# Output projection of a hybrid attention and mLSTM layer: seven block products by Strassen's scheme instead of eight

## The chip, the cores and the metric

One NeuronCore of a Trainium2 chip. The metric is the device time of one execution in microseconds. The engines are named as the profile names them: PE (TensorE), DVE (VectorE), ACT (ScalarE), POOL (GpSimd), SP (SyncE, whose queue issues the DMAs here).

## The reference

A pre-RMSNorm layer on 4096 tokens of 1024 channels, in float32. One input projection feeds two groups of heads: stick-breaking attention (8 heads of 64) and mLSTM (4 heads of 128). Each branch is multiplied by a SiLU gate; the two are concatenated to `mix` (4096 x 1024). What the change touches is only the end:

```python
mix = jnp.concatenate([sb_out, ml_out], axis=-1)
h = h + mix @ w_out[layer].astype(mix.dtype)      # 4096x1024 @ 1024x1024
return rms_norm(h, final_norm_g)
```

## The kernel before

The program works through four sweeps over the tokens and then the output projection. Two sweeps do attention, two do mLSTM (two heads each); a sweep has 8 blocks of 512 tokens. An attention block has 8 slots, an mLSTM block 10. In an mLSTM block the slots 0 to 5 each hold one `t_quantum` (24 float16 matmuls of 512 columns), slots 6 to 9 each two `n_mm` groups (48 matmuls of 256 columns). All big products are split products: each operand is a high and a low part, and three of the four part products are summed (high x high, low x high, high x low).

The order is written out by hand. `at(slot, phase, fn)` hangs a function on the phase "pre", "mid" or "post" of a slot, `run` calls what hangs there, and each engine executes its own instructions in exactly the order in which they are issued. So an instruction that waits holds up everything behind it on its engine. Slot 0 of the projection is `c_g`, the last mLSTM block begins at `gl = c_g - 10`; work of a block trails into the next one's slots (`m2`, `m3`, `m3b`, `m4` of a block run in slots 0 to 5 of the next).

In those trailing slots DVE has a chain that TensorE waits for when it is late. In slot 2 `fin_conv` multiplies three times (L778); `m3` computes per-token statistics, on which POOL builds `rs` (L879, L880); in slot 3 `m3b` normalises (L886, four instructions), then come the next three multiplies, and in slot 4 `m4` transposes the first head on TensorE (L894) into the one PSUM buffer "at" and DVE reads it with the gate (L896). The second head's transposes in slot 5 need that buffer back, and all matmuls of the slot stand behind them. POOL meanwhile has the splits of weights (`split`, L251; `Prep.lows`, L314).

The projection (line 1125) takes a token tile of 128 rows and one half of the 1024 output columns at a time: 8 k-tiles x 3 part products = 24 matmuls of 512 columns with float32r operands, into one of two PSUM buffers "pj". `c_add` adds the result to x (L1130, DVE) and squares it for the norm (L1131, ACT). `c_norm` (L1170, L1171, POOL) makes the factor, `c_out` (L1178, DVE) scales the two halves and SP stores the tile. `m_load` fetches `mix` from the DRAM scratch `scr_m`, `m_split` makes its two parts (L250 ACT, L251 DVE). The weights are loaded and split in eight pieces in the last mLSTM block (`wo_load`: ACT and POOL, 1,024 wide, slots 2 to 9). The last tile's second half is done in two pieces of 256 columns (`c_last`) so that little is left behind the last matmul.

Of the kernel before, what the change touches and what calls it, by code (L numbers as in the profile page):

```python
# [43 lines left out]
def hymba_kernel(ctx: ExitStack, tc: tile.TileContext, x, norm_g, w_in, b_ig, b_fg, conv_w,
                 conv_b, hn_g, w_out, fn_g, out):
    nc = tc.nc
    x2, out2 = x[0], out[0]
# [151 lines left out]
def main_pass(ctx, tc, x2, norm_g, win, win_k, b_ig, b_fg, conv_w, conv_b, hn_g, wout_k, fn_g,  # L199
              out2, scr_u, scr_m, scr_M, scr_E, flag):  # L200
# [848 lines left out]
    WO = {}  # L1049
    gl = ml_g(2 * NB - 1)  # L1050

    def wo_load(i):
        box = []

        def ld():
            r = stage()
            half, k0 = (1, 2 * i) if i < 4 else (0, 2 * i - 8)
            SP.dma_start(out=r.rearrange("p (k c) -> p k c", k=2), in_=wout_k[:, k0:k0 + 2, 512 * half:512 * half + 512])
            box.append(r)

        def sp():
            key = ("ba"[i // 4], i % 4)
            if i < 6:
                WO[key] = [wp.tile([128, DM], F32R, tag="wT", name="wT", bufs=T_SLOTS) for _ in range(2)]
# [29 lines left out]
    mt = {}  # L1094

    def m_load(i):
        if i < 4:
            t = stage().rearrange("p (k t) -> p k t", k=KT)
            SP.dma_start(out=t, in_=scr_m[i])
            for j in range(2):  # L1100
                mt[i, j] = t[:, 4 * j:4 * j + 4, :]
            return
        for j in range(2):
            t = ph_tile("z", [128, 4, 128])
            SP.dma_start(out=t, in_=scr_m[i, :, 4 * j:4 * j + 4, :])
            mt[i, j] = t

    mb = {}

    def m_split(i):  # L1110
        if i // 2 not in mb:
            mb.pop(i // 2 - 2, None)
            mb[i // 2] = up.tile([128, 2, 2, KT, 128], F32R, tag="U", name="U", bufs=2)
        u = mb[i // 2][:, i % 2]
        for j in range(2):
            ks = slice(4 * j, 4 * j + 4)
            split(u[:, 0, ks, :], u[:, 1, ks, :], mt.pop((i, j)))

    def c_mm(ps, i, half, c0, n, mid=None):
        u = mb[i // 2][:, i % 2]  # L1120
        for k in range(KT):
            wh, wl = WO["ab"[half], k // 2]
            cs = slice((k % 2) * 512 + c0, (k % 2) * 512 + c0 + n)
            for j, (a, w) in enumerate(((0, wh), (1, wh), (0, wl))):
                PE.matmul(ps, u[:, a, k, :], w[:, cs], start=(k == 0 and j == 0), stop=(k == KT - 1 and j == 2))  # L1125
            if k == 3 and mid:
                mid()

    def c_add(ps, hsl, sq):
        V.tensor_tensor(out=hsl, in0=ps, in1=hsl, op=ALU.add)  # L1130
        A.activation(out=ph_tile("kl0", list(hsl.shape)), in_=hsl, func=AF.Square, scale=DM ** -0.5, accum_out=sq)  # L1131

    def c_quantum(g, i, half):
        run(g, "pre")
        ps = ps_tile("pj", [128, 512])
        c_mm(ps, i, half, 0, 512, lambda: run(g, "mid"))
        if i not in hs2:
            hs2[i] = sm.tile([128, 2], F32, tag="hs2", name="hs2", bufs=3)
        c_add(ps, xt[i][:, half * 512:(half + 1) * 512], hs2[i][:, half:half + 1])
        run(g, "post")  # L1140

    def c_last(g):

        run(g, "pre")
        i = NT - 1
        t, sq = xt.pop(i), hs2.pop(i)
        last = sm.tile([128, 1], F32, tag="ss", name="ss")
        y = ph_tile("kl1", [128, 512])
        for c0, dst in ((0, sq[:, 0:1]), (256, last)):
            ps = ps_tile("pj", [128, 256])  # L1150
            c_mm(ps, i, 0, c0, 256)
            c_add(ps, t[:, c0:c0 + 256], dst)
            if c0 == 0:
                G.tensor_scalar(out=sq[:, 0:1], in0=sq[:, 0:1], scalar1=sq[:, 1:2], scalar2=EPS, op0=ALU.add, op1=ALU.add)
                G.tensor_tensor(out=t[:, 512:1024], in0=t[:, 512:1024], in1=fng[1], op=ALU.mult)
            V.tensor_tensor(out=y[:, c0:c0 + 256], in0=t[:, c0:c0 + 256], in1=fng[0][:, c0:c0 + 256], op=ALU.mult)
        V.tensor_tensor(out=last, in0=last, in1=sq[:, 0:1], op=ALU.add)
        G.tensor_tensor(out=last, in0=last, in1=mhalf[:, 0:1], op=ALU.pow)
        V.tensor_scalar(out=y, in0=y, scalar1=last, scalar2=None, op0=ALU.mult)
        SP.dma_start(out=out2[i * 128:(i + 1) * 128, 0:512], in_=y)  # L1160
        A.activation(out=t[:, 512:1024], in_=t[:, 512:1024], func=AF.Copy, scale=last)
        SP.dma_start(out=out2[i * 128:(i + 1) * 128, 512:1024], in_=t[:, 512:1024])
        run(g, "mid")
        run(g, "post")

    def c_norm(i):
        t = xt[i]
# [4 lines left out]
        xt[i] = (t, ss)  # L1172

    def c_out(i):
# [4 lines left out]
        SP.dma_start(out=out2[i * 128:(i + 1) * 128, :], in_=t)  # L1179


    with tc.manual_schedule():
# [146 lines left out]
        seq = [(0, 1), (1, 1), (0, 0), (1, 0)]  # L1329
        for i in range(2, NT):  # L1330
            seq += [(i, 1), (i, 0)]
        where = {ih: n for n, ih in enumerate(seq)}
        load_fng()
        for i in range(NT):
            n = max(where[i, 0], where[i, 1])
            n_first = min(where[i, 0], where[i, 1])
            at(c_g + max(n_first - 2, 0), "pre", lambda i=i: x_load(i))
            if i < NT - 1:
                at(c_g + n + 1, "pre", lambda i=i: c_norm(i))
                at(c_g + n + 2, "pre", lambda i=i: c_out(i))  # L1340
            if i >= 4:
                at(c_g + 2 * i - 6, "pre", lambda i=i: m_load(i))
                at(c_g + 2 * i - 4, "mid", lambda i=i: m_split(i))

# [6 lines left out]
        for n, (i, half) in enumerate(seq[:-1]):  # L1351
            c_quantum(c_g + n, i, half)
        c_last(c_g + len(seq) - 1)
        for g in range(c_g + len(seq), c_g + len(seq) + 4):
# [31 lines left out]
```

## Time and profile before

| | |
|---|---|
| median of 3 timed runs | 2305.04 us (2304.14 to 2309.72) |
| profiled execution | 2303.64 us, of it 2301.9 us span |
| PE busy | 2211.8 us (96%), granted clock 0.986 in the mean |
| DVE, ACT, POOL busy | 1319.9, 1007.7, 719.3 us (57%, 44%, 31%) |

These lines of the page cut the span into 40 equal slices (57.5 us each); a digit is the busy share in tenths. The projection is the last six to seven slices.

```profile
PE   4699999999999999999999999999999999999998
PEld 3366566666666666567767665666667677888887
DVE  6477777756666666755555555654544445433332
ACT  3477667656666666533333333222333334222221
POOL 2277667754555556511111112200000013100000
PEclk7899999999999999999999999999999999999999
DMA  6244444411111122112222232221222224444442
```

TensorE is busy nearly everywhere, the other engines have room, and the DMA engines too. An engine's busy share does not say whether its next instruction comes in time for another engine; that is read from the timeline.

### The profile page before, as it was taken

Reading aid. Unit: us, or ns where it says so; the run is one execution under the profiler, and the core shown is the slowest. Engines: PE = TensorE matmul, PEld = TensorE weight load, DVE = VectorE, ACT = ScalarE, POOL = GpSimd, SP = SyncE. Lnnn points to the kernel's source line nnn. Section 1 sums busy time; section 2 is a strip of 40 time slices with the busy share of each in tenths; the row PEclk is TensorE's granted clock in tenths of the full one; section 3 lists DMA queues with packets and bytes.
Section 4 is the critical chain, followed back from the end, with each engine's and each line's share of the span. In section 5 each row is a group of like instructions: output and inputs, shape, how many; then the busy total and the mean of one; then the engine's idle time right before and its main releaser. Section 6 shows DMA issues by size and latency. Waiting matters only on the chain.

```text
span 2301.9 us, 36279 instructions
## 1 busy us (share of the span) xinstructions
PE 2211.8 (96%) x13945; PEld 1526.6 (66%) x13945; DVE 1319.9 (57%) x2725; ACT 1007.7 (44%) x1806; POOL 719.3 (31%) x1134
## 2 busy tenths in 40 slices
PE   4699999999999999999999999999999999999998
PEld 3366566666666666567767665666667677888887
DVE  6477777756666666755555555654544445433332
ACT  3477667656666666533333333222333334222221
POOL 2277667754555556511111112200000013100000
PEclk7899999999999999999999999999999999999999
DMA  6244444411111122112222232221222224444442
GB/s 184 52 90 93 93 98 97 112 46 47 65 57 56 56 67 84 59 51 74 74 74 74 74 92 47 65 65 57 60 55 65 61 74 138 146 138 150 152 137 93
DMA packets 221917, 193.98 MB, mean 84 GB/s; under 512 B 108084, under 2 KB 177768, under 8 KB 221736
## 3 DMA queue, kind: packets, MB, share of 16 engines
q1 hardware_dynamic: 221720, 191.59, 29.4%
q8 instruction: 111, 1.82, 0.3%
q14 instruction: 70, 0.57, 0.1%
q10 hardware_dynamic: 16, 0.00, 0.0%
HBM read 141.09 MB, written 50.46 MB: 83 GB/s over the span
## 4 chain that ended last, share of the span: by engine, by line
PE 73%; DVE 6%; issue 1%; ACT 1%; DMA 0%; POOL 0%; POOLq 0%; DVEq 0%; ACTq 0%
PE ps_pj L480 31%; PE ps_pj L492 17%; PE ps_pj L1125 15%; PE ps_zu L823 1%; DVE z L778 1%; PE ps_at L617 1%; PE ps_o L633 1%; PE ps_zu L866 1%; PE ps_zu L867 1%; DVE c L738 1%; PE ps_at L824 1%; PE ps_o L848 1%; PE ps_zu L848 1%; PE ps_at L894 1%; PE ps_zu L586 1%
## 5 line engine op out<-in xcount | busy, mean ns | idle before, releaser
L480 PE MATMUL ps_pj<-U,wT 128*128 128x512 f16 x4608 | 1045.0, 382 | 0.0
L480 PEld LDWEIGHTS <-wT 128*128 128x128 f16 x4608 | 452.5, 99 | 494.4 <-issue 11.4
L492 PEld LDWEIGHTS <-U 128*128 128x128 f16 x4608 | 452.1, 98 | 82.8 <-DVE kl L565 11.9
L492 PE MATMUL ps_pj<-wna,U 128*128 128x256 f16 (+1 forms) x3072 | 361.7, 276 | 17.4 <-DVE kl L565 7.5
L1125 PE MATMUL ps_pj<-wT,U 128*128 128x512 f32 (+1 forms) x1164 | 267.8, 387 | 0.0
L1125 PEld LDWEIGHTS ps_pj<-wT,U 128*128 128x128 f32 x1164 | 216.6, 188 | 44.3
L601 POOL TENSOR_TENSOR sA<-sA,bP 128x510 f32<-128x510 f32 x128 | 151.7, 1185 | 199.2 <-DVE bP L600 180.4
L600 DVE TENSOR_TENSOR_SCAN bP<-bP,D 128x512 f32<-128x512 f32 x128 | 162.9, 1273 | 53.1 <-POOL bP L592 52.9
L492 PE MATMUL ps_pj<-wnb,U 128*128 128x256 f16 x1536 | 178.1, 273 | 0.0
L1131 ACT ACTIVATE kl<-st 128x512 f32<-128x512 f32 (+1 forms) x65 | 40.7, 625 | 274.1 <-DVE st L1130 265.8
L879 POOL TENSOR_SCALAR rs<-mv 128x4 f32<-128x4 f32 x32 | 8.0, 250 | 483.7 <-DVE kl L773 448.4
L774 ACT ACTIVATE kl<-ps_pj,SC 128x512 f32<-128x512 f32 x64 | 44.0, 687 | 242.0 <-PE ps_pj L480 208.9
L1130 DVE TENSOR_TENSOR st<-ps_pj,st 128x512 f32<-128x512 f32 (+1 forms) x65 | 44.4, 683 | 173.9 <-PE ps_pj L1125 170.7
L825 DVE TENSOR_TENSOR bP<-ps_zu,bP 128x512 f32<-128x512 f32 x32 | 22.1, 691 | 203.5 <-PE ps_at L824 202.4
L778 DVE SCALAR_TENSOR_TENSOR z<-kl,CT,z 128x512 f32<-128x512 f32 x144 | 118.3, 821 | 19.8 <-ACT z L775 15.2
L622 DVE SCALAR_TENSOR_TENSOR ATl<-ps_at,ATh 128x512 f16<-128x512 f32 (+1 forms) x128 | 87.8, 686 | 41.3 <-ACT ATh L621 39.2
L810 POOL TENSOR_SCALAR_AFFINE_SELECT bP<-bP 128x512 f32<-128x512 f32 x32 | 24.3, 760 | 270.0 <-DVE bP L809 239.8
L787 ACT ACTIVATE v<-ps_pj,SC 128x256 f32<-128x256 f32 x64 | 30.3, 474 | 168.8 <-PE ps_pj L492 168.2
L1170 POOL TENSOR_SCALAR ss<-hs 128x1 f32<-128x1 f32 x31 | 9.6, 311 | 292.3 <-ACT kl L1131 292.3
L563 ACT ACTIVATE kh<-ps_pj 64x512 f16<-64x512 f32 x128 | 75.6, 590 | 57.4 <-PE ps_pj L480 39.1
L1125 PE MATMUL ps_pj<-wna,U 128*128 128x512 f32 (+1 forms) x396 | 92.8, 383 | 0.0
L537 ACT ACTIVATE zml<-ps_pj,SC 128x512 f32<-128x512 f32 x32 | 22.0, 687 | 159.8 <-DMA scr_m<-zml 144.8
(233 smaller groups left out, 3458.8 us busy)
## 6 DMA issues: line engine op xcount, KB each, us to landing
U<-scr_u SPq DMA_DIRECT2D x96, 512.0 KB
st<-in_x_dram SPq DMA_DIRECT2D x40, 512.0 KB
scr_u<-U SPq DMA_DIRECT2D x32, 512.0 KB
out_dram<-st SPq DMA_DIRECT2D x31, 512.0 KB
st<-in_w_in_dram SPq DMA_DIRECT2D x28, 512.0 KB
z<-scr_m SPq DMA_DIRECT2D x56, 256.0 KB
st<-in_x_dram SPq DMA_DIRECT2D x96, 128.0 KB
scr_m<-z SPq DMA_DIRECT2D x32, 256.0 KB
```

Of the source, the lines that this page charges most:

```text
L480: PE.matmul(p3, wt[:, a, k, :], u[:, :, b, k, :], start=(k == 0 and i == 0), stop=(k == KT - 1 and i == 2))
L492: PE.matmul(ps[:, c0:c0 + n], u[:, a, k, :], w[:, b, k, 0:n], start=first and j == 0, stop=last and j == len(order) - 1)
L563: A.activation(out=kh[d, h, 128:640], in_=ps[e], func=AF.Copy, scale=S_QKV)
L600: V.tensor_tensor_scan(out=bf, data0=bf, data1=D1[:, ::-1], initial=1.0, op0=ALU.mult, op1=ALU.max)
L601: G.tensor_tensor(out=sg[:, :, 0:255], in0=sg[:, :, 0:255], in1=b[:, :, 1:256], op=ALU.mult)
L622: V.scalar_tensor_tensor(out=l[:, i:, :], in0=ps[:, i:, :], scalar=S_A, in1=h[:, i:, :], op0=ALU.mult, op1=ALU.subtract)
L774: A.activation(out=raw[:, 3:515], in_=ps, func=AF.Copy, scale=inv(sid))
L778: V.scalar_tensor_tensor(out=y, in0=raw[:, t:t + 512], scalar=CT[:, 8 * t + grp:8 * t + grp + 1], in1=y, op0=ALU.mult, op1=ALU.add)
L848: PE.matmul(ps[:, j, :], mK[hh][:, c, :], vaug(p0 + c, hh), start=True, stop=True)
L1125: PE.matmul(ps, u[:, a, k, :], w[:, cs], start=(k == 0 and j == 0), stop=(k == KT - 1 and j == 2))
L1130: V.tensor_tensor(out=hsl, in0=ps, in1=hsl, op=ALU.add)
L1131: A.activation(out=ph_tile("kl0", list(hsl.shape)), in_=hsl, func=AF.Square, scale=DM ** -0.5, accum_out=sq)
```

## The change

Tokens are taken in pairs of tiles. The two tiles and the two halves of k make a 2 x 2 block matrix A, the two halves of k and of the output columns a 2 x 2 block matrix B. Winograd's form of Strassen's scheme multiplies seven pairs of blocks (each 4 k-tiles x 3 part products = 12 matmuls of 512 columns, now float16) where the plain way multiplies eight. It needs sums of blocks:

- of the weights, once: `wo_top` reads all of w_out and takes its largest entry (slots 0 to 17 of the second mLSTM sweep, `g3`), `wo_build` reads it again, scales it, forms four sums on POOL and splits seven operands into float16 parts, a quarter in each of four mLSTM blocks (from slot `g3 + 20`). Four operands stay in SBUF, three go out to `scr_w` and come back by `tw_load`.
- of `mix`, per pair: four maxima (`m_top`, DVE), the scale (`m_bound`: one matmul with an all-ones matrix on PE that sums the row maxima over the partitions, then small DVE steps), four scalings (ACT), four sums (POOL), seven high parts (ACT), seven low parts (three DVE, four POOL).

A product is added where it belongs as soon as its PSUM bank holds the right partial sum; three banks per pair are in use, and a bank goes on accumulating after it has been read. `c_add` now multiplies by the pair's inverse scale on the way (seven per pair). The step list `seq` puts the last product of a pair behind the first of the next; `atp(t, fn)` hangs a function ahead of step t, half a slot each. `c_last` is gone, and so is the pass of float32r splits. The stage pool has 6 buffers instead of 5.

```diff
-    WO = {}
     gl = ml_g(2 * NB - 1)
-    def wo_load(i):
...
+    g3 = ml_g(NB)
+    def total_top(src, n, top, out_scale, out_back, back):
+        ps = ps_tile("zu", [128, 8])
+        PE.matmul(ps[:, 0:n], ones, src, start=True, stop=True)
+        mx = sm.tile([128, 1], F32, tag="wx", name="wx")
+        V.tensor_reduce(out=mx, in_=ps[:, 0:n], op=ALU.max, axis=AX.X)
+        V.tensor_scalar(out=mx, in0=mx, scalar1=1e-30, scalar2=1.0 / top, op0=ALU.max, op1=ALU.mult)
+        V.reciprocal(out=out_scale, in_=mx)
+        V.tensor_scalar(out=out_back, in0=mx, scalar1=back, scalar2=None, op0=ALU.mult)
+    def wo_top(i):
...
+        at(g3 + 2 * i, "pre", ld)
+        at(g3 + 2 * i + 1, "mid", lambda: V.tensor_reduce(out=wom[:, i:i + 1], in_=box.pop(), op=ALU.max, axis=AX.X,
+                                                         apply_absolute_value=True))
...
+    def wo_build(j, g):
...
+        def combine(i):
...
+                G.tensor_tensor(out=t1, in0=b12, in1=b11, op=ALU.subtract)
+                G.tensor_tensor(out=t2, in0=b22, in1=t1, op=ALU.subtract)
...
+                G.tensor_tensor(out=t3, in0=b22, in1=b12, op=ALU.subtract)
+                G.tensor_tensor(out=t4, in0=b21, in1=ops[3], op=ALU.subtract)
...
+        def low(os):
+            for o in os:
+                h, l = parts(o)
+                G.tensor_tensor(out=l, in0=ops[o], in1=h, op=ALU.subtract)
...
+        at(g, "pre", ld)
+        at(g + 2, "pre", lambda: scale(0))
+        at(g + 2, "mid", lambda: scale(1))
+        at(g + 3, "pre", lambda: combine(0))
+        at(g + 3, "post", lambda: combine(1))
+        at(g + 3, "mid", lambda: high((0, 2, 4)))
+        at(g + 5, "pre", lambda: high((1, 3)))
+        at(g + 5, "mid", lambda: high((5, 6)))
+        for i, o in enumerate(((0, 2), (4, 1), (3, 5), (6,))):
+            at(g + 4 + i, "post", lambda o=o: low(o))
+        at(g + 9, "pre", put)
+    for j in range(4):
+        wo_build(j, g3 + 20 + ML_SLOTS * j)
...
+    def m_top(p):
+        un[p] = sm.tile([128, 6], F32, tag="mtop", name="mtop", bufs=4)
+        for i, t in enumerate(mt[p]):
+            V.tensor_reduce(out=un[p][:, i:i + 1], in_=t.rearrange("p k t -> p (k t)"), op=ALU.max, axis=AX.X,
+                            apply_absolute_value=True)
+    def m_bound(p):
+        u = un[p]
+        total_top(u[:, 0:4], 4, M_TOP, u[:, 4:5], u[:, 5:6], SO[:, 1:2])
...
+    def m_combine(p):
...
+        G.tensor_tensor(out=s1, in0=a21, in1=a22, op=ALU.add)
+        G.tensor_tensor(out=s2, in0=s1, in1=a11, op=ALU.subtract)
+        G.tensor_tensor(out=s4, in0=a12, in1=s2, op=ALU.subtract)
+        G.tensor_tensor(out=s3, in0=a11, in1=a21, op=ALU.subtract)
...
+    def m_low(p, os):
+        for o in os:
+            (V if o in (0, 2, 6) else G).tensor_tensor(out=mo[p][:, o, 1], in0=mt[p][o], in1=mo[p][:, o, 0], op=ALU.subtract)
+    def c_product(p, o, ps, first, last):
+        a, (wh, wl) = mo[p][:, o], TW[o]
+        for k in range(4):
+            for i, (l, r) in enumerate(((0, wh), (1, wh), (0, wl))):
+                PE.matmul(ps, a[:, l, k, :], r[:, k, :], start=first and k == 0 and i == 0, stop=last and k == 3 and i == 2,
+                          skip_group_check=True)
+    def c_add(p, ps, i, half):
+        t = xt[2 * p + i][:, half * 512:(half + 1) * 512]
+        V.scalar_tensor_tensor(out=t, in0=ps, scalar=un[p][:, 5:6], in1=t, op0=ALU.mult, op1=ALU.add)
...
+    seq = []
+    for p in range(NP):
+        seq += [(p, 0), (p - 1, 6)] if p else [(p, 0)]
+        seq += [(p, o) for o in ((1, 2, 3, 4, 5) if p < NP - 1 else (1, 3, 2, 5, 4, 6))]
...
+        t0 = where[p, 0]
+        for i in (2 * p, 2 * p + 1):
+            atp(t0 - 5, lambda i=i: x_load(i))
+        atp(t0 - 13, lambda p=p: m_load(p))
+        atp(t0 - 9, lambda p=p: m_top(p))
+        atp(t0 - 8, lambda p=p: m_bound(p))
+        atp(t0 - 7, lambda p=p: m_scale(p, (2, 3)))
+        atp(t0 - 7, lambda p=p: m_scale(p, (0, 1)))
+        atp(t0 - 6, lambda p=p: m_combine(p))
+        atp(t0 - 5, lambda p=p: m_high(p, (0, 2, 6)))
+        atp(t0 - 4, lambda p=p: m_low(p, (0, 2, 6)))
+        atp(t0 - 4, lambda p=p: m_high(p, (1, 3)))
+        atp(t0 - 3, lambda p=p: m_low(p, (1, 3)))
+        atp(t0 - 3, lambda p=p: m_high(p, (4, 5)))
+        atp(t0 - 2, lambda p=p: m_low(p, (4, 5)))
+        n = where[p, 4] + 1 if p == NP - 1 else where[p, 5] + 1
+        atp(n, lambda p=p: c_norm(2 * p))
+        atp(n + 1, lambda p=p: c_out(2 * p))
+        n = where[p, 6] + 1
+        atp(n, lambda p=p: c_norm(2 * p + 1))
+        atp(n + 1, lambda p=p: c_out(2 * p + 1))
...
+            run(c_g + n // 2, "mid" if n % 2 else "pre")
+            c_step(p, o)
```

## Rows read from the trace of the kernel before

**Rows 1.** Windows: start and end, length, busy us and count per engine, clock, DMA share.
```profile
...
1938.40:2292.90 354.50, 354.50 (x1613) 294.86 (x1611) 138.85 (x239) 78.12 (x192) 34.92 (x69) 1.00 0.42 140
...
```

**Rows 2.** Timeline in the projection: start, length, instruction, idle time before it.
```profile
...
2104.96 2.88 PE L1125 MATMUL ps_pj<-wna,U 128*128 128x512 f32 x12
...
2107.68 8.32 PE L1125 MATMUL ps_pj<-wT,U 128*128 128x512 f32 x36
2107.88 0.69 DVE L1130 TENSOR_TENSOR st<-ps_pj,st 128x512 f32<-128x512 f32 x1 [3.43 <-PE ps_pj L1125]
...
2115.84 2.88 PE L1125 MATMUL ps_pj<-wna,U 128*128 128x512 f32 x12
...
```

**Rows 3.** Chain of waits: start, length, what, how many instructions.
```profile
...
1908.99 5.18 PE ps_pj L480 x24
...
```

**Rows 4.** Timeline, last mLSTM block, slots 2 to 5.
```profile
...
1895.63 4.30 DVE L778 SCALAR_TENSOR_TENSOR z<-kl,CT,z 128x512 f32<-128x512 f32 x3
1896.60 5.54 POOL L251 TENSOR_TENSOR wT<-st,wT 128x1024 fp32r<-128x1024 f32 x2
...
1899.85 5.19 DVE L886 TENSOR_SCALAR ATl<-ATl,mv,rs 128x128 f32<-128x128 f32 x4
...
1902.60 2.36 POOL L251 TENSOR_TENSOR wT<-st,wT 128x1024 fp32r<-128x1024 f32 x1 [0.46 <-ACT wT L250]
...
1908.34 0.66 PE L894 MATMUL ps_at<-idf,ATl 128*128 128x128 f32 x4 [3.52 <-DVE zml L896]
...
```

**Rows 5.** Timeline, first block of the second mLSTM pass.
```profile
...
1468.75 5.04 POOL L314 TENSOR_TENSOR wnb<-st,wnb 128x1024 f16<-128x1024 f32 x2
...
1478.07 0.66 PE L894 MATMUL ps_at<-idf,ATl 128*128 128x128 f32 x4 [1.40 <-DVE zml L896]
...
```

**Rows 6.** Single lines: count, ns min/median/max, first and last start, form.
```profile
...
L284 PE MATMUL ps_zu<-idf,wmb x25: 272/273/477, 69.4 to 1448.2; 128*128 128x128 f32 x25
...
L273 DVE TENSOR_REDUCE wm<-ATh x4: 676/676/679, 32.2 to 68.0; 128x4 f32<-128x512 f32 x4
...
L601 POOL TENSOR_TENSOR sA<-sA,bP x128: 1087/1089/1920, 105.0 to 974.2; 128x510 f32<-128x510 f32 x128
...
```

**Rows 7.** Groups by line and form: busy us, mean ns, idle before.
```profile
...
L251 DVE TENSOR_TENSOR U<-z,U 128x512 fp32r<-128x512 f32 x56 | 36.2, 688 | 37.0 <-ACT U L250 37.0
...
L1178 DVE SCALAR_TENSOR_TENSOR st<-st,ss,O 128x512 f32<-128x512 f32 x31 | 23.1, 746 | 0.0
...
L1131 ACT ACTIVATE kl<-st 128x512 f32<-128x512 f32 x63 | 39.8, 632 | 269.9 <-DVE st L1130 261.6 <-issue 8.2
...
L1131 ACT ACTIVATION_READ_ACCUMULATOR kl<-st 128x1 f32 x65 | 12.1, 186 | 0.0
...
L1171 POOL TENSOR_TENSOR ss<-ss,mhalf 128x1 f32<-128x1 f32 x31 | 17.7, 570 | 2.6
...
L1170 POOL TENSOR_SCALAR ss<-hs 128x1 f32<-128x1 f32 x31 | 9.6, 311 | 292.3 <-ACT kl L1131 292.3
...
L297 POOL TENSOR_TENSOR wT<-ATh,wT 128x512 f16<-128x512 f32 x3 | 3.5, 1153 | 5.9 <-ACT wT L296 5.9
...
```

**Rows 8.** Timeline, a block in which POOL has no splits.
```profile
...
1651.90 2.33 DVE L778 SCALAR_TENSOR_TENSOR z<-kl,CT,z 128x512 f32<-128x512 f32 x3
...
1654.14 1.11 DVE L886 TENSOR_SCALAR ATl<-ATl,mv,rs 128x128 f32<-128x128 f32 x4
...
```

**Rows 9.** Timeline of TensorE at the end of the first mLSTM pass.
```profile
...
1412.43 1.11 PE L894 MATMUL ps_at<-idf,ATl 128*128 128x128 f32 x4 [5.64 <-DVE zml L896]
1413.33 7.92 PE L480 MATMUL ps_pj<-U,wT 128*128 128x512 f16 x24
...
```

**Rows 10.** Windows behind that wait (columns as in rows 1).
```profile
...
1416.00:1418.00 2.00, 2.00 (x6) 0.65 (x5) 0.94 (x2) 0.00 (x0) 0.00 (x0) 0.50 0.04 11
...
```

**Rows 11.** Timeline, the last store.
```profile
...
2293.15 0.42 DVE L1130 TENSOR_TENSOR st<-ps_pj,st 128x256 f32<-128x256 f32 x1 [1.99 <-PE ps_pj L1125]
...
2296.08 0.90 SPq L1162 DMA_DIRECT2D out_dram<-st  x1
...
```

More of the change, by code (lines that the diff above doesn't have):

```diff
@@ L40 @@
 S_A = 2.0 ** 15
+M_TOP = 8192.0
 @with_exitstack
@@ L54, in hymba_kernel @@
     scr_m = dram.tile([NT, 128, KT, 128], F32, name="scr_m")
+    scr_w = dram.tile([3, 128, 2, 4, 512], F16, name="scr_w")
     scr_M = dram.tile([ML_H, SEQ], F32, name="scr_M")
@@ L247, in main_pass @@
     D1 = const.tile([128, 512], F32, name="D1")
+    ones = const.tile([128, 128], F32, name="ones")
+    wom = const.tile([128, 8], F32, name="wom")
+    SO = const.tile([128, 2], F32, name="SO")
     def split(h, l, src, eng_l=None):
@@ L1056, in ld @@
             r = stage()
-            half, k0 = (1, 2 * i) if i < 4 else (0, 2 * i - 8)
-            SP.dma_start(out=r.rearrange("p (k c) -> p k c", k=2), in_=wout_k[:, k0:k0 + 2, 512 * half:512 * half + 512])
+            SP.dma_start(out=r, in_=wout_k[:, i, :])
             box.append(r)
[L1061 to L1064, printed above, removed]
-            else:
-                t = wp.tile([128, 2 * DM], F32R, tag="wna", name="wna", bufs=2)
-                WO[key] = [t[:, 0:DM], t[:, DM:2 * DM]]
-            split(*WO[key], box.pop(), G)
@@ L1080, in main_pass, with tw_load @@
+    for j in range(4):
+        wo_build(j, g3 + 20 + ML_SLOTS * j)
+    def tw_load(o):
+        t = [wp.tile([128, 4, 512], F16, tag="wT", name="wT", bufs=T_SLOTS) for _ in range(2)]
+        for i in range(2):
+            SP.dma_start(out=t[i], in_=scr_w[o - 4, :, i])
+        TW.append(t)
+    for o in (4, 5, 6):
+        at(gl + 2 * o - 5 if o < 6 else gl + 6, "pre", lambda o=o: tw_load(o))
     fng = [None, None]
@@ L1092, in x_load @@
         xt[i] = t
[L1094 to L1099, printed above, removed]
-            for j in range(2):
[L1101 to L1164, printed above, removed]
@@ new lines, in main_pass, with m_load @@
+    NP = NT // 2
+    mt, mo, un = {}, {}, {}
+    def m_load(p):
+        mt[p] = []
+        for i in (2 * p, 2 * p + 1):
+            if p < 2:
+                t = stage().rearrange("p (k t) -> p k t", k=KT)
+                SP.dma_start(out=t, in_=scr_m[i])
+                mt[p] += [t[:, 0:4, :], t[:, 4:8, :]]
+                continue
+            for j in range(2):
+                t = ph_tile("zv"[p % 2], [128, 4, 128])
+                SP.dma_start(out=t, in_=scr_m[i, :, 4 * j:4 * j + 4, :])
+                mt[p].append(t)
@@ new lines, in m_top, with m_scale @@
+    def m_top(p):
[6 more added lines that the diff above has]
+        total_top(u[:, 0:4], 4, M_TOP, u[:, 4:5], u[:, 5:6], SO[:, 1:2])
+    def m_scale(p, js):
+        for j in js:
+            A.activation(out=mt[p][j], in_=mt[p][j], func=AF.Copy, scale=un[p][:, 4:5])
@@ new lines, in m_high @@
+    def m_high(p, os):
+        if p not in mo:
+            mo[p] = up.tile([128, 7, 2, 4, 128], F16, tag="U", name="U", bufs=2)
+        for o in os:
+            A.activation(out=mo[p][:, o, 0], in_=mt[p][o], func=AF.Copy)
+    def m_low(p, os):
+        for o in os:
+            (V if o in (0, 2, 6) else G).tensor_tensor(out=mo[p][:, o, 1], in0=mt[p][o], in1=mo[p][:, o, 0], op=ALU.subtract)
+    cps = {}
+    def c_product(p, o, ps, first, last):
[4 more added lines that the diff above has]
+                          skip_group_check=True)
@@ new lines, in c_add, with c_square @@
+    def c_add(p, ps, i, half):
+        t = xt[2 * p + i][:, half * 512:(half + 1) * 512]
+        V.scalar_tensor_tensor(out=t, in0=ps, scalar=un[p][:, 5:6], in1=t, op0=ALU.mult, op1=ALU.add)
+    def c_square(p, i, half):
+        t = 2 * p + i
+        if t not in hs2:
+            hs2[t] = sm.tile([128, 2], F32, tag="hs2", name="hs2", bufs=4)
+        A.activation(out=ph_tile("kl0", [128, 512]), in_=xt[t][:, half * 512:(half + 1) * 512], func=AF.Square, scale=DM ** -0.5,
+                     accum_out=hs2[t][:, half:half + 1])
@@ new lines, in c_done, with c_step @@
+    def c_done(p, ps, i, half):
+        c_add(p, ps, i, half)
+        c_square(p, i, half)
+    def c_step(p, o):
+        if o == 0:
+            cps[p] = [ps_tile(tag, [128, 512]) for tag in ("pj", "o", "zu")]
+        b1, b2, b3 = cps[p]
+        if o == 0:
+            c_product(p, o, b1, True, False)
+            c_add(p, b1, 0, 0)
+        elif o == 1:
+            c_product(p, o, b2, True, False)
+            c_add(p, b2, 1, 1)
+        elif o == 2:
+            c_product(p, o, b3, True, True)
+            c_done(p, b3, 0, 0)
+        elif o == 3:
+            c_product(p, o, b1, False, False)
+            c_add(p, b1, 0, 1)
+        elif o == 4:
+            c_product(p, o, b2, False, True)
+            c_done(p, b2, 0, 1)
+        elif o == 5:
+            c_product(p, o, b1, False, False)
+            c_done(p, b1, 1, 1)
+        else:
+            c_product(p, o, b1, False, True)
+            c_done(p, b1, 1, 0)
@@ L1166, in c_norm @@
     def c_norm(i):
-        t = xt[i]
         ss = sm.tile([128, 1], F32, tag="ss", name="ss")
@@ L1204, in main_pass @@
         G.memset(D1, 0.0)
+        G.memset(ones, 1.0)
         G.memset(D1[:, 255:256], 1.0)
@@ L1327, in main_pass @@
                     run(gi, "post")
[L1329 to L1343, printed above, removed]
+        at(c_g + 2, "post", load_fng)
         def flag_max(src, dst, n):
@@ L1350, in main_pass @@
         at(c_g + 9, "mid", lambda: flag_max(accT, flag, 1))
[L1351 to L1354, printed above, removed]
+        for n, (p, o) in enumerate(seq):
+            run(c_g + n // 2, "mid" if n % 2 else "pre")
+            c_step(p, o)
+            if n % 2:
+                run(c_g + n // 2, "post")
+        for g in range(c_g + len(seq) // 2, c_g + len(seq) // 2 + 4):
             for phase in ("pre", "mid", "post"):
```

75 lines of the change are left out of this document (60 added, 15 removed).

## The prediction

> **What bounds the kernel now.** I read the page's engine totals first (the table above): TensorE is busy for 96% of the span, so only what shortens TensorE's queue, or makes it wait, counts. Then the busy time by stage: from the first matmul of the output projection to its last there are 354.50 us with TensorE busy in all of them, while DVE has 138.85, ACT 78.12 and POOL 34.92 [rows 1]. The timeline inside that stage gives the pace: 48 matmuls (one token tile) from 2104.96 to 2115.84, 0.2267 us each [rows 2]. The chain of waits has 24 float16 matmuls of the same 512 columns in 5.18 us, 0.2159 each [rows 3]. Last, the places where TensorE does wait, because the change adds work just there [rows 4, 5].
>
> **The products.** Before: 31 token tiles of 48 matmuls and a last one whose four column pieces count as 48 full ones, 1,536 x 0.2267 = 348.2 us; the other 6.3 of the 354.5 are small matmuls of the last mLSTM block, which stay. After: 16 pairs x 7 products x 12 matmuls = 1,344 x 0.2159 = 290.2 us. Gain 58.0: 192 fewer matmuls, and float16 instead of float32r. A product lasts 12 x 0.2159 = 2.59 us, a pair 18.14. Weight loads stay hidden, as they do beside the float16 matmuls now.
>
> **The bound of a pair (m_top, m_bound).** The new thing on TensorE's queue is the all-ones matmul of `total_top`. It stands between two products and needs four maxima that DVE issues just one product earlier. Nothing hides a late maximum: all matmuls are queued behind it. A small float32 matmul is 0.27 us long [rows 6], of which some 0.16 lies under its neighbour, as with the others (12 matmuls are 2.88 long at a pace of 12 x 0.2267 = 2.72) [rows 2]: 16 x 0.11 = 1.8, and between nothing and 4.3.
>
> The wait, lower end: DVE starts 0.20 after a product's end (2107.68 to 2107.88) [rows 2]; the queue holds first `c_add` of product 3, about 0.65 to the next operation, then four maxima of 512 (0.68 long, some 0.61 from one to the next) [rows 6], then some 0.1 to TensorE: 0.20 + 0.65 + 2.5 + 0.1 = 3.45 us against 2.59. TensorE waits 0.9 us per pair even when DVE comes to it with an empty queue.
>
> It does not come with an empty queue. I follow the queues from the start of product 5 of one pair (t = 0), with the durations of [rows 2, 6, 7] and about 0.1 for a semaphore. Its sum is written at 2.8 to 3.4, squared by 4.3 (0.63 and 0.19 for the accumulator). Only then can ACT scale the next pair's four blocks, 4.3 to 6.6 (four of 512, priced like the square). POOL's four sums take 1.15 each from 5.5 on; DVE's two output halves (`c_out`, 0.75 each) fall among them, so they end at about 11.5. The second tile's `c_norm` is queued behind them on POOL: 0.3 and 0.57, 12.4. Only now can DVE write that tile's two output halves, and POOL has in the meantime begun a low part: DVE 13.5 to 14.9, then three low parts (0.69) to 16.7, the sums of products 2 and 3 to 18.0, the four maxima to 20.5. TensorE was ready for them at 18.1. So it waits 2.4 us. One collision more or less of DVE with POOL is worth about 0.85 (below), so I put the wait between 0.9 and 3.3 and take 2.4, the sum with the collisions that the queue order brings. Pairs 0 and 1 have their bound ahead of the stage, where DVE has time; 14 x 2.4 = 33.6 (12.6 to 46).
>
> **DVE against POOL.** An operation of DVE with both inputs in SBUF, or a copying one, does not run beside POOL's two-input work. In the last mLSTM block three POOL operations of 2.36 us meet DVE: three multiplies take 4.30 instead of 2.33 and four normalising steps 5.19 instead of 1.11, 6.05 us lost, 2.0 per POOL operation, or 0.85 of it [rows 4, 8]. POOL loses too: 1.92 us at most against 1.089 [rows 6]. Maxima keep their 676 to 679 ns [rows 6], so I count them as untouched, and so the sums out of PSUM.
>
> **Building the weight operands (wo_build).** Four mLSTM blocks get it. Four POOL sums in slot 3 and three low parts stand back to back in POOL's queue behind the normaliser, and meet the same DVE chain: multiplies, normalising, multiplies, then the gated output for which the transposes of the second head wait. The block that has such a burst now loses 3.52 us of TensorE (three operations, 6.05 lost on DVE) [rows 4]: about 2.5 of slack. Another, with two operations of together 5.04, loses 1.40 [rows 5]. Seven operations of 1.15 at 0.8 to 0.95 each lose DVE 5.6 to 6.7, less the slack 3.1 to 4.2: I take 3.7 per block, 14.8 in four. Lower end, where the low parts come too late to meet the chain: 4 x 0.85 - 2.5 = 0.9, 3.6 in four. Upper end under the third rival. The burst that costs 3.52 today goes with the old splits: -3.5.
>
> **wo_top.** Eight maxima of 1,024 (1.2 us each, a little under twice the 0.68) [rows 6] in the first two blocks of that pass. The first has the loss of 1.40 already, so two of them ahead of its chain add 2.4; in the second they fall into the slack. +2.4 (0 to 5). The second read of the weights (4 MB more, and 6 MB out and back) lies on queues that the page's slices show busy for some two tenths of the time in that pass.
>
> **The end.** Today the add after the last matmul starts at 2293.15 and the last store is issued by 2296.98 [rows 11]: pieces of 256, scaled on two engines. Then: add of 512 (0.69), square (0.82), two POOL steps (0.87), two output halves in a row (1.5), waits between: some 4.7 instead of 3.8, and 512 KB of the tile before still ahead on the queue, about 1 us. +1.8 (0 to 4). Shorter prologue or longer: one memset more, nothing.
>
> **The sum.** -58.0 + 33.6 + 1.8 + 14.8 - 3.5 + 2.4 + 1.8 = -7.1. The profiled execution took 2303.64 (span 2301.9 and 1.7 around it), 1.4 under the median of the timed runs: 2303.6 - 7.1 = 2296.5.
>
> **Rivals.**
> 1. The collisions miss. POOL's sums and DVE's stores slip past each other, the bound waits 0.9, the low parts miss the chain in the builds. For it: DVE has 18 operations of some 0.65 us per pair and the small ones, 12 us of 19. Against it: the order of the queues is fixed and repeats alike in each pair. -58.0 + 12.6 + 1.8 + 3.6 - 3.5 + 2.4 + 1.8 = -39.3, 2264.
> 2. No wait at the bound at all, because the maxima are early: 12.6 less, 2252. Against it: the lower end above has nothing but row durations.
> 3. Slower: the builds drop TensorE's clock. Place: slot 5 of four blocks. If a POOL operation holds DVE off for its whole length, seven cost 8.05, less 2.5 is a wait of 5.6 us. After a wait of 5.64 the granted clock is 0.50, the lower of the two levels, still at 1416 to 1418, and the 24 matmuls are 7.92 long: against 5.18 from start to start, some 5.3 long, 2.6 more, 3.0 with the transposes ahead of them (1.11 for 0.66) [rows 4, 9, 10]. After the wait of 3.52 the 24 took the 5.18 [rows 3, 4]. It decides somewhere between the two. Then 4 x 8.6 = 34.4 instead of 14.8, and in the projection four collisions per pair, each 0.15 dearer, make 14 x 3.0 = 42 of the 33.6: -7.1 + 19.6 + 8.4 = +20.9, 2324.5. For it: the wait lies near. Against it: 0.85 in the rows.
>
> The Trainium skill, SBUF — State Buffer, section "SBUF: two separate sides", speaks for the third: DVE and GpSimd take their shared port pair as an exclusive lock for the whole instruction, and the loser fully blocks. The trace agrees that they block, but with 2.0 of 2.36 us. By the rule the time is that of the third rival, 2324.5.
>
> **How the numbers follow.** Forecast 0.50, own range 2284 to 2308 (the builds at 1.5 to 4.5, the bound at 2.0 to 2.9); first rival 0.22; second 0.08; third 0.20. 0.3% is 6.9 us, about what a measurement of this kernel tells from no change: faster means under 2298, slower over 2312. Just over half of the forecast (0.27) and rivals 1 and 2 with little lost give 0.55 faster; the rest of the forecast and the near edge of the third 0.24 the same; 0.21 slower. Range 2262 to 2325: to the first and the third rival; the second and the far half of the third stay out, 0.18.
>
> **What would show it.** The projection, first product to last, about 333 us; 14 gaps on TensorE of 2 to 3 us ahead of the ones matmul, released by DVE's maximum, 20.6 us apart. In four blocks a gap of about 3.7 us ahead of L894's transposes at the full clock. Wrong if the gaps are under 1 us, if the clock shows 0.5 there, or if products of one pair wait for each other.

## The result, and the profile after

The changed kernel takes 2336.31 us (median, 2334.64 to 2339.4) against 2305.36 in the same comparison: ratio 1.013, interval 1.0118 to 1.0142. A second comparison gave 1.015 (1.0133 to 1.0167). It is slower, and the time lies outside the range that I gave.

The profiled execution has a span of 2332.8 us, 30.9 more than before and 38.0 more than forecast (2301.9 - 7.1 = 2294.8). Lines of the changed kernel stand five lower than before as far as the mLSTM code goes (L894 is L899). The page of the changed kernel:

```profile
PE 2184.6 (94%) x13763; PEld 1379.9 (59%) x13763; DVE 1472.9 (63%) x2894; ACT 1085.5 (47%) x1943; POOL 928.7 (40%) x1298
...
PE   5699999999999999999999999999999999888887
...
```

TensorE has 27.2 us less to do (2211.8 before), yet the span is longer: it now stands idle, and the slices show it in the last six, the projection. By stage the windows of the changed kernel (columns as in [rows 1]: the projection, then what comes behind the last matmul):

```profile
1963.70:2323.00 359.30, 316.72 (x1423) 143.22 (x1420) 248.08 (x379) 133.20 (x289) 189.18 (x183) 0.96 0.38 130
2323.00:2332.80 9.80, 0.14 (x1) 0.00 (x0) 3.49 (x5) 0.72 (x2) 1.32 (x3) 0.72 0.30 115
```

The projection starts 25.3 us later than before (1938.4 [rows 1]; forecast 13.7 later), lasts 359.3 us (354.5 before, forecast 331.9: 354.5 - 58.0 + 33.6 + 1.8) and is followed by 9.8 us (9.0 before, forecast 10.8). The errors are +11.6, +27.4 and -1.0, together the 38.0.

**The projection.** What TensorE waited for there (who waits, whom for, total us, times, longest):

```profile
PE ps_zu L1060 <- DVE mtop L1198: 39.6, 13, 3.2
PE ps_pj L1239 <- DVE st L1244: 2.9, 2, 2.2
```

So 42.5 us of waits against 33.6. The rest is that 316.72 us are busy where 298.3 were forecast (290.2 + 6.3 + 1.8). One pair in the changed kernel's timeline, from product 5 to the next ones matmul, shows both:

```profile
2144.60 7.93 PE L1239 MATMUL ps_pj<-wT,U 128*128 128x512 f16 x36
...
2150.25 1.27 POOL L1217 TENSOR_TENSOR sA<-v 128x512 f32<-128x512 f32 x1 [3.43 <-ACT v L1207]
...
2154.84 1.28 POOL L1220 TENSOR_TENSOR sA<-v 128x512 f32<-128x512 f32 x1
...
2157.19 0.75 DVE L1295 SCALAR_TENSOR_TENSOR st<-st,ss,yx 128x512 f32<-128x512 f32 x1 [1.28 <-POOL ss L1288]
2157.38 3.14 POOL L1231 TENSOR_TENSOR U<-sA,U 128x512 f16<-128x512 f32 x2 [0.22 <-ACT U L1227]
...
2159.42 2.84 DVE L1231 TENSOR_TENSOR U<-v,U 128x512 f16<-128x512 f32 x3
...
2163.51 2.45 DVE L1198 TENSOR_REDUCE mtop<-z 128x1 f32<-128x512 f32 x4
...
2166.01 0.38 PE L1060 MATMUL ps_zu<-mtop,ones 128*128 128x4 f32 x2 [3.12 <-DVE mtop L1198]
2166.26 9.62 PE L1239 MATMUL ps_pj<-wT,U 128*128 128x512 f16 x36
```

The queues run nearly as worked out: POOL's sums from 5.7 to 11.5 us after the start of product 5, the output halves from 12.6 (13.5 in the prediction), the low parts from 14.8 (14.9). But the three low parts on DVE take 2.84 us instead of 2.07 (3 x 0.69), and POOL's low parts run beside them; the maxima end 0.9 later than forecast and the ones matmul waits 3.12. Then comes what the forecast does not have: the 36 matmuls behind the wait take 9.62 us, not 7.93. The window of the changed kernel behind another such wait (3.11) has a mean granted clock of 0.60, near 0.50, the lower of the two levels; in the one after it the clock is back at 0.99:

```profile
2097.80:2101.80 4.00, 3.98 (x12) 1.60 (x13) 1.12 (x5) 0.72 (x2) 1.46 (x3) 0.60 0.00 0
2101.80:2110.00 8.20, 8.20 (x39) 3.78 (x38) 5.18 (x5) 3.24 (x7) 4.45 (x3) 0.99 0.04 15
```

Eight of the thirteen ones matmuls are followed by such a stretch (9.62 or 9.63 for 36), five are not (7.93): 1.69 us each time. The eight waited 3.11 to 3.21 us, the five 2.71 to 3.01. A ninth stretch of half clock follows a wait of 2.17 us of product 6 of the first pair: 4.44 us for 12 matmuls instead of 2.75, again 1.69.

**The builds.** One of the four blocks with a build, and what follows, in the changed kernel's timeline:

```profile
1663.13 4.86 DVE L891 TENSOR_SCALAR ATl<-ATl,mv,rs 128x128 f32<-128x128 f32 x4
...
1666.74 2.27 POOL L1136 TENSOR_TENSOR wT<-st,wT 128x512 f16<-128x512 f32 x2
1667.91 1.13 DVE L778 COPY kl<-halo 128x3 f32<-128x3 f32 x1
1668.97 1.15 POOL L1136 TENSOR_TENSOR O<-st,O 128x512 f16<-128x512 f32 x1
1669.14 1.00 DVE L781 COPY halo<-kl 128x3 f32<-128x3 f32 x1
...
1673.10 1.12 PE L899 MATMUL ps_at<-idf,ATl 128*128 128x128 f32 x4 [3.90 <-DVE zml L901]
1674.00 7.69 PE L485 MATMUL ps_pj<-U,wT 128*128 128x512 f16 x24
```

The normalising takes 4.86 us (1.11 undisturbed [rows 8]), and even copies of three columns are held for about a microsecond. The four waits are 4.21, 3.90, 3.92 and 3.90, 15.9 in all where 14.8 were forecast. But behind each the transposes take 1.11 or 1.12 us, and the 24 matmuls 7.25, 7.69, 7.90 and 6.33 instead of 5.34: 9.6 us more.

### The profile page after: what moved, and what is told of

Its sections match the earlier page's. It is cut to its first block, busy times and chain, and to the rows that moved or that the text cites. A ratio compares the mean times of both kernels' runs of the same rounds, so it can differ in the third digit from the quotient of the medians.

```text
span 2332.8 us, 36362 instructions
## 1 busy us (share of the span) xinstructions
PE 2184.6 (94%) x13763; PEld 1379.9 (59%) x13763; DVE 1472.9 (63%) x2894; ACT 1085.5 (47%) x1943; POOL 928.7 (40%) x1298
## 4 chain that ended last, share of the span: by engine, by line
PE 58%; DVE 13%; issue 4%; POOL 4%; ACT 2%; DMA 0%; POOLq 0%; DVEq 0%; ACTq 0%
PE ps_pj L485 29%; PE ps_pj L497 17%; DVE U L1231 2%; DVE z L783 2%; DVE st L1295 1%; PE ps_pj L1239 1%; DVE mtop L1198 1%; PE ps_zu L828 1%; PE ps_o L638 1%; PE ps_at L622 1%; DVE ATl L891 1%; PE ps_zu L871 1%; PE ps_zu L872 1%; POOL sA L1218 1%; POOL sA L1219 1%
## 5 line engine op out<-in xcount | busy, mean ns | idle before, releaser
L497 PEld LDWEIGHTS <-U 128*128 128x128 f16 x4608 | 453.4, 99 | 81.5 <-issue 11.3
L1239 PEld LDWEIGHTS <-U 128*128 128x128 f16 x1344 | 135.5, 102 | 168.6 <-issue 23.8
L1250 ACT ACTIVATE kl<-st 128x512 f32<-128x512 f32 x64 | 40.3, 630 | 227.1 <-issue 133.2
L1239 PE MATMUL ps_pj<-wT,U 128*128 128x512 f16 x576 | 142.6, 411 | 2.9 <-DVE st L1244 2.9
L783 DVE SCALAR_TENSOR_TENSOR z<-kl,CT,z 128x512 f32<-128x512 f32 x144 | 120.9, 839 | 19.5 <-ACT z L780 14.9
L1231 POOL TENSOR_TENSOR U<-sA,U 128x512 f16<-128x512 f32 x56 | 74.9, 1357 | 57.3 <-ACT U L1227 57.3
L1244 DVE SCALAR_TENSOR_TENSOR st<-ps_pj,mtop,st 128x512 f32<-128x512 f32 x64 | 47.5, 744 | 72.1 <-PE ps_pj L1239 72.1
L595 ACT ACTIVATE sA<-ps_zu,SX 128x512 f32<-128x512 f32 x128 | 88.2, 689 | 0.0
```

Source lines behind the costliest of these rows:

```text
L497: PE.matmul(ps[:, c0:c0 + n], u[:, a, k, :], w[:, b, k, 0:n], start=first and j == 0, stop=last and j == len(order) - 1)
L595: A.activation(out=sg, in_=z, func=AF.Sigmoid, scale=SX[:, s, pair, 0:1])
L783: V.scalar_tensor_tensor(out=y, in0=raw[:, t:t + 512], scalar=CT[:, 8 * t + grp:8 * t + grp + 1], in1=y, op0=ALU.mult, op1=ALU.add)
L1231: (V if o in (0, 2, 6) else G).tensor_tensor(out=mo[p][:, o, 1], in0=mt[p][o], in1=mo[p][:, o, 0], op=ALU.subtract)
L1239: PE.matmul(ps, a[:, l, k, :], r[:, k, :], start=first and k == 0 and i == 0, stop=last and k == 3 and i == 2, skip_group_check=True)
L1244: V.scalar_tensor_tensor(out=t, in0=ps, scalar=un[p][:, 5:6], in1=t, op0=ALU.mult, op1=ALU.add)
```

## The experiments

Theory A: the time goes into two kinds of waits of TensorE, each from the place where DVE's and POOL's instructions stand in their queues, and into the half clock that follows many of these waits. The rivals, by experiment: one of DVE's own load, of POOL's sums alone, of a clock lowered by something other than the waits, or of losses with a common cause. Times stand against the kernel before in the same comparison (2308.13 us for the first four, 2305.61 for the others); "against the changed kernel" is the difference of the ratios times 2305. A ratio's interval stands behind it.

**The bound one slot later.**

```diff
-        atp(t0 - 8, lambda p=p: m_bound(p))
+        atp(t0 - 7, lambda p=p: m_bound(p))
```

> Only edit: m_bound stands one product later in TensorE's queue (behind product 5 of the pair, not behind product 4). Theory A (TensorE waits for the place of the bound, and the half-speed clock comes from those waits): the maxima come about 3.0 us after product 4, a product lasts 2.59, so the 13 waits shrink from 3.0 to about 0.4 us each (39.6 to some 6 in all) and no stretch behind them shows the clock at 0.50 (13 us): 2336 - 34 - 13 = about 2290. Rival B (the projection is bound by the chain of DVE, ACT and POOL from pair to pair, and the bound is only where it shows): a product then waits for its low part or its bank instead, the projection stays at 350 us or more and the time above 2325.

Measured: 2291.13 us, 0.9928 (0.9911 to 0.9944), some 46 us below the changed kernel. One product more lies between the maxima and the ones matmul; its waits are gone, and what is left is a short wait of product 5 for the sum of product 3 (fourteen of the fifteen; the first is product 6's). Two views of this kernel: its waits from the start of the second mLSTM sweep on, and its window from the first product to the end:

```profile
PE ps_at L899 <- DVE zml L901: 19.6, 5, 4.2
PE ps_pj L1239 <- DVE st L1244: 14.2, 15, 2.1
```

```profile
1965.70:2290.20 324.50, 300.20 (x1424) 140.26 (x1423) 254.65 (x384) 134.49 (x292) 193.32 (x187) 0.99 0.43 147
```

The same window of the changed kernel:

```profile
1963.70:2332.80 369.10, 316.85 (x1423) 143.22 (x1420) 251.57 (x384) 133.92 (x291) 190.50 (x185) 0.95 0.38 130
```

The same matmuls, 316.85 us against 300.20. Of these 16.65 us the nine stretches at half clock make 9 x 1.69 = 15.2; the other 1.4 are the thirteen ones matmuls, which take 0.25 us from start to start behind a wait and 0.14 without one. The waits give 42.5 - 14.2 = 28.3. The sum, 45, is the gain that was measured, within its interval. And 300.20 lies within 2 us of the forecast 298.3: the products cost what I said.

**The weight build four slots later.** Scales, sums and parts move past the end of the DVE chain for which the transposes wait.

```diff
-        at(g + 2, "pre", lambda: scale(0))
-        at(g + 3, "pre", lambda: combine(0))
-        at(g + 3, "post", lambda: combine(1))
...
+        at(g + 6, "pre", lambda: scale(0))
+        at(g + 6, "post", lambda: combine(0))
+        at(g + 7, "post", lambda: combine(1))
...
```

> Only edit: the weight operands are scaled, summed and split in slots 6 to 9 of the same four blocks (behind POOL's masks) instead of slots 2 to 7. Theory A (POOL's back-to-back sums hold off DVE's two-input work in slots 2 to 4, and the transposes of the second head wait): the four waits of 3.9 to 4.2 us go, and with them the four stretches at clock 0.50 (2.7 us or so each): 2336 - 16 - 11 = about 2309. Rival C (the four blocks lose by ACT's extra scaling and high parts or by the DMA traffic, wherever they stand): less than 8 us gained.

Measured: 2316.75 us, 1.0035 (1.0023 to 1.0046), 22 below the changed kernel. The build waits are gone, and the projection starts at 1944.1, 19.6 earlier; its own waits stay (thirteen from that start on, 41.4 us in all, against 39.6):

```profile
PE ps_zu L1060 <- DVE mtop L1198: 42.5, 15, 4.6
PE ps_at L899 <- DVE zml L901: 3.6, 1, 3.6
```

The 3.6 is block 8, the first of the second mLSTM sweep, where `wo_top` stands. From its transposes to the first product this kernel needs 460.2 us, the changed kernel 484.3: 24.1 less, although here half clock follows the 3.6 (transposes and 24 matmuls of 1.11 and 6.39 us instead of 0.66 and 5.34: 1.5 more), which it does not in the changed kernel. Together 25.6, the 15.9 of waits and the 9.6 of half clock that stood in the builds.

**Work in the wait.** Twelve float16 matmuls whose result nobody reads stand ahead of the ones matmul.

```diff
+        if p >= 3:
+            fill = ps_tile("at", [128, 512])
+            for i in range(12):
+                PE.matmul(fill, mo[p - 2][:, 0, 0, i % 4, :], TW[0][0][:, i % 4, :], start=(i == 0), stop=(i == 11))
```

> Only edit: 12 float16 matmuls whose result nobody reads stand ahead of the bound's matmul for the pairs from 3 on, so that TensorE works 2.6 of the 3.0 us that it waits. Theory A: the maxima come when they came, so nothing is later, and the clock stays at 1.00 because the idle stretch is under 0.6 us: 7 or 8 falls of 1.7 us each go, 2336 - 13 = about 2323. Rival D (the half-speed stretches have another cause than the idle time): the same time as before this edit, 2336, and as many stretches at 0.50.

Measured: 2326.36 us, 1.0073 (1.0057 to 1.009), 13 below the changed kernel, though TensorE does 156 matmuls more. Waits and window of this kernel:

```profile
PE ps_zu L1060 <- DVE mtop L1198: 10.0, 15, 2.8
```

```profile
1971.40:2328.10 356.70, 337.16 (x1580) 155.07 (x1578) 252.45 (x384) 134.08 (x291) 189.88 (x184) 0.99 0.39 134
```

Without the fill (35.8 us busy) 301.4 remain, nearly as in the first experiment. Behind the twelve waits of 0.52 to 0.62 us that are left ahead of the ones matmuls the clock no longer falls; the one stretch at half clock that remains in the stage follows the wait of 2.17 of product 6. All other work of the stage is what it was, so the eight falls came from TensorE standing idle.

**Without POOL's sums.** The four sums of `m_combine` are left out, and the parts are taken from the blocks themselves.

```diff
-        G.tensor_tensor(out=s1, in0=a21, in1=a22, op=ALU.add)
...
-        mt[p] = [a11, s1, a12, s2, s4, s3, a22]
+        mt[p] = [a11, a21, a12, a22, a12, a11, a22]
```

> The four sums of mix blocks per pair are left out (products 1, 3, 4 and 5 take plain blocks instead), all else as in the changed kernel. Theory A (POOL's four sums push the second tile's norm factor, that pushes DVE's stores and low parts, and these push the maxima): the wait at the bound falls from 3.0 to about 1.0 us per pair and the clock stays at 1.00: 2336 - 28 - 13 = about 2295. Rival E (the maxima are late because they follow the sum of product 3 by queue order alone, POOL does not matter): the wait stays above 2.4 us and the time above 2325.

Measured: 2307.01 us, 0.9999 (0.9989 to 1.001), 30 below the changed kernel; the wait is 1.8 per pair, not the 1.0 expected, and one of the thirteen is followed by half clock. In this kernel's timeline the reason stands: the low parts of DVE still meet those of POOL.

```profile
2117.36 2.85 POOL L1222 TENSOR_TENSOR U<-z,U 128x512 f16<-128x512 f32 x2 [1.12 <-ACT U L1218]
...
2119.12 2.84 DVE L1222 TENSOR_TENSOR U<-z,U 128x512 f16<-128x512 f32 x3
```

So the sums make 1.3 of the 3.0 us. By the rows the collision of the low parts makes another 0.8 (2.84 for some 2.07), which leaves 1.0, near the 0.9 that the forecast had for maxima that meet an empty queue; no run took these two apart.

**The changed kernel again,** as the measure for the three that follow.

> The changed kernel unaltered, as the measure for the three beside it on this chip. Both theories: 1.013 times the kernel before, as in the first comparison, with four waits of about 4 us ahead of the mLSTM transposes and thirteen or fourteen of about 3 us ahead of the ones matmul.

Measured: 2339.07 us, 1.015 (1.0133 to 1.0167).

**Only the low parts of the build later.**

```diff
-        for i, o in enumerate(((0, 2), (4, 1), (3, 5), (6,))):
-            at(g + 4 + i, "post", lambda o=o: low(o))
-        at(g + 9, "pre", put)
+        for o, w8 in (((0, 2), (8, "pre")), ((4, 1), (8, "post")), ((3, 5), (9, "mid")), ((6,), (9, "post"))):
+            at(g + w8[0], w8[1], lambda o=o: low(o))
+        at(g + 11, "pre", put)
```

> The seven low parts of each weight block move three to four slots later; the four sums and the seven high parts stay where they were. Theory A (each of GpSimd's operations that runs beside VectorE's chain to zml takes its own share of VectorE, and the half clock comes from the wait that this adds up to): three of the seven operations that lie beside the chain leave it, the waits ahead of the transposes fall from 3.9-4.2 us to 1.4-2.1 us, no clock fall follows them, and the projection starts 4 x (2.0 + 2.7) = 19 us earlier: about 19 us below the changed kernel of the same comparison (15 to 24). Rival (the four sums alone make the wait, the lows find VectorE between instructions): waits still above 3 us, the clock still falls, and at most 4 us come back.

Measured: 2323.58 us, 1.0074 (1.0055 to 1.0094), some 17 below the changed kernel. In its timeline the wait is short and the clock full:

```profile
1664.42 3.99 DVE L891 TENSOR_SCALAR ATl<-ATl,mv,rs 128x128 f32<-128x128 f32 x4
...
1668.34 0.16 DVE L778 COPY kl<-halo 128x3 f32<-128x3 f32 x1
...
1671.71 0.66 PE L899 MATMUL ps_at<-idf,ATl 128*128 128x128 f32 x4 [1.23 <-DVE zml L901]
1672.21 5.34 PE L485 MATMUL ps_pj<-U,wT 128*128 128x512 f16 x24
```

Three POOL operations less beside the chain take 2.7 us from the wait (3.90 to 1.23), 0.9 each: the price of a collision was about right. The four sums, which stayed, still hold the normalising at 3.99 us instead of 1.11.

**Both edits,** the bound one slot later and the build four.

> The bound one slot later and the whole weight build four slots later, together. Theory A (both losses come from waits in different places, so that they add): the first edit alone gave about -45 us against the changed kernel and the second about -20, so -62 to -67 for both, about 0.984 to 0.987 of the kernel before; no wait ahead of the ones matmul, none ahead of the transposes, fifteen short waits of about 1 us of a product for the sum of the fourth product. Rival (a common cause, such as a clock lowered by the work of the stage as a whole, or a build that collides with what now runs late): the sum of both is missed by over 15 us, above 0.992.

Measured: 2269.37 us, 0.9835 (0.9819 to 0.9852), some 73 below the changed kernel, where the two edits alone add up to 68; with intervals of several microseconds that is the same. The losses add, and this version is faster than both kernels, by 1.65% (1.48 to 1.81) against the one before. What is left in it from the start of the second mLSTM sweep on is the 3.6 in block 8 and the 15.1 us of short waits, nearly all of product 5:

```profile
PE ps_pj L1239 <- DVE st L1244: 15.1, 15, 2.7
```

**Both, and product 3 ahead of product 2,** so that two products lie between 3 and 5, which share a bank.

```diff
-    seq += [(p, o) for o in ((1, 2, 3, 4, 5) if p < NP - 1 else ...
+    seq += [(p, o) for o in ((1, 3, 2, 4, 5) if p < NP - 1 else ...
```

> As the run with both edits, and in each pair the fourth product comes ahead of the third, so that two products, not one, lie between the fourth and the sixth, which share one bank of PSUM. Theory A (the remaining 1-us wait is the sixth product's, for the sum that empties that bank and stands on VectorE behind three low parts): the fifteen waits go, the period of a pair comes down from 19.2 to 18.2-18.4 us, and the time is 11 to 15 us below the run with both edits, about 0.979 of the kernel before. Rival (VectorE's queue sets the period, so that a wait comes back in another place): a wait of the ones matmul or of a product takes its place, and the time is within 4 us of the run with both edits.

Measured: 2296.3 us, 0.9961 (0.9947 to 0.9976), 29 above the version with both edits. My theory had the right wait, the sum behind the three low parts, but the other order did not shorten it: TensorE now waits 29.7 us for sums (15.1 before), and four of these waits are followed by half clock. The rival, which expected no gain, was too mild. Its timeline:

```profile
2104.35 6.27 POOL L1231 TENSOR_TENSOR U<-sA,U 128x512 f16<-128x512 f32 x4 [0.22 <-ACT U L1227]
...
2106.41 4.76 DVE L1231 TENSOR_TENSOR U<-z,U 128x512 f16<-128x512 f32 x3
...
2111.09 0.74 DVE L1244 SCALAR_TENSOR_TENSOR st<-ps_pj,mtop,st 128x512 f32<-128x512 f32 x1
...
2111.88 2.75 PE L1239 MATMUL ps_pj<-wT,U 128*128 128x512 f16 x12 [2.18 <-DVE st L1244]
```

The sum of product 3 still stands on DVE behind the three low parts, and now all four of POOL's low parts run beside those: 4.76 us instead of 2.84. Product 3 was done earlier, the queue in front of its sum grew longer. Whether another order of the low parts would take the last 15 us away was not tried.

## Why the prediction was wrong

- **The products** (-58.0): right. Free of waits and of the half clock TensorE needs 300.20 us from the first product to the end; the terms gave 298.3.
- **DVE against POOL** (0.85 per operation of POOL): about right, 0.9 us measured. The prediction works 0.85 out as a share of an operation's length and then uses it as microseconds; as a share of 1.15 it would be 0.98, 7 x 0.98 - 2.5 = 4.4 us per block, and 3.9 to 4.2 were measured. The third rival's price, each operation's whole length, wanted waits of 5.6 us. The Trainium skill, SBUF — State Buffer, section "SBUF: two separate sides", has the lock last for the whole instruction, and the trace of the changed kernel agrees: the small copy of DVE that starts at 1669.14, behind POOL's operation of 1668.97 to 1670.12, ends at 1670.14. It is held to the end of that operation, but it came 0.17 us into it and would have needed another 0.17, so it loses less than the whole length.
- **The builds' waits** (14.8): 15.9, right. **wo_top** (+2.4): block 8 waits 3.62 instead of 1.40 [rows 5], right. The old wait of 3.52 is gone, right.
- **The bound's wait** (2.4 x 14 = 33.6): 42.5, within its bounds and too small. Thirteen waits of 3.0 make 39.6 of it, two of products 2.9. The mis-sized term is "three low parts (0.69) to 16.7": they collide with POOL's low parts, take 2.84 us and end at 17.7.
- **The clock**: the step that failed. I put nothing behind the forecast's waits, 2.4 in the projection and 3.7 in the builds (these "at the full clock"), because the wait of 3.52 before was not followed by a fall [rows 3, 4], and asked for a point "somewhere between the two", 3.52 and 5.64. There is no such point. The clock fell at nine waits of 2.17 to 3.21 us in the projection, which cost 15.2 us, and at the four in the builds, which cost 9.6: 25 of the 38 us of error. The waits' own sizes are another 10 (8.9 and 1.1). The clock at 0.5 in the builds was one of the prediction's own signs of being wrong.

The trace of the kernel before already spoke against that point, in a place that the prediction did not look at, where the attention sweeps pass into the first mLSTM sweep: a wait of 3.24 us, shorter than the 3.52, with the granted clock at 0.50 behind it (timeline and window of the kernel before; the 24 matmuls of 256 columns take 2.78 us at the full clock):

```profile
982.01 0.26 PE L633 MATMUL ps_o<-ATl,v 128*128 128x128 f16 x1 [3.24 <-DVE halo L772]
...
982.92 3.83 PE L492 MATMUL ps_pj<-wna,U 128*128 128x256 f16 x24
```

```profile
982.00:984.00 2.00, 1.99 (x11) 1.62 (x11) 1.27 (x4) 1.92 (x4) 0.00 (x0) 0.50 0.01 5
```

The third rival had the right kind of loss at the right place in the builds, but put it behind waits that did not come, and had no half clock in the projection, where most of it fell.

The forecast's sign hung on that, but not on that alone: the profiled span of 2332.8 us less the 24.8 of half clock is 2308, still 6 above the kernel before. By my own sum, -58 and some 51 us of waits, 7 us of gain were left, and the waits' sizes alone took 10. Two slips in the sums change nothing: the range of 2284 to 2308 is laid around the median of the timed runs (2305), the forecast of 2296.5 around the profiled execution, 1.4 lower; and the projection of "about 333 us" is 331.9 by the terms.

## What to carry to other kernels

A change that takes matmuls away and puts a wait in every round is to be priced with two terms per wait: its length, and the slower matmuls behind it (here 1.4 to 3.0 us). One wait in the old trace that went without the second is no evidence for the next, and here a shorter one in the same trace had it. A quantity that TensorE needs once per round is asked for a whole product later than it seems to be ready, and work that two engines fight over goes behind the chain that TensorE waits for: here these two moves of a few lines turned a loss of 1.5% into a gain of 1.65%, both measured in one comparison.

## What the runs showed of the hardware

The length of a wait alone does not tell whether the clock falls. At one and the same instruction, the transposes of block 8, the changed kernel waits 3.62 us and goes on at the full clock, the version with both edits waits 3.61 and does not (each timeline in that order):

```profile
1479.29 0.66 PE L899 MATMUL ps_at<-idf,ATl 128*128 128x128 f32 x4 [3.62 <-DVE zml L901]
1479.78 5.34 PE L485 MATMUL ps_pj<-U,wT 128*128 128x512 f16 x24
```

```profile
1485.14 1.11 PE L899 MATMUL ps_at<-idf,ATl 128*128 128x128 f32 x4 [3.61 <-DVE zml L901]
1486.05 7.64 PE L485 MATMUL ps_pj<-U,wT 128*128 128x512 f16 x24
```

Of the nine profiled executions that have this wait, at 3.60 to 3.64 us, six show half clock behind it. The wait of 3.23 to 3.25 us between attention and mLSTM has it in all ten profiled executions, the builds' waits of 3.90 to 4.21 in all twenty cases.

In the kernel with product 3 ahead of product 2, ten waits are 2.16 to 2.19 us long; three of them are followed by a fall, the others are not:

```profile
2047.28 2.75 PE L1239 MATMUL ps_pj<-wT,U 128*128 128x512 f16 x12 [2.19 <-DVE st L1244]
...
2068.45 4.43 PE L1239 MATMUL ps_pj<-wT,U 128*128 128x512 f16 x12 [2.19 <-DVE st L1244]
```

Waits of 0.82 us (both edits) and those of 1.23 to 1.36 (low parts later) were not followed by one; the shortest that was, in these traces from the end of the attention sweeps to the last matmul, is 1.76 (without POOL's sums, one of thirteen). The Trainium skill, TensorE: Matmul & The Clock Gate, section "HAM oscillation — how this bites in real kernels", describes idle gaps in each round that lower the clock again and again; the trace agrees, eight falls in thirteen rounds. What else, beside the length, decides about a single wait, these runs leave open.
